# A gated MLP's width-3 convolution: its two neighbour terms moved from VectorE to GpSimd and one accumulating transfer, with one prefetch buffer given up

## The chip, the cores and the metric

The kernel runs on one NeuronCore of a Trainium2 chip. It is one launch, and the metric is the device time of that launch in microseconds (us). TensorE is PE in the profile (its weight loads are PEld), VectorE is DVE, ScalarE is ACT, GpSimd is POOL and SyncE is SP. A measurement of this kernel can tell about 0.2% (4.5 us) from no change.

## The reference

The model is two layers of a bidirectional encoder on 256 positions of width 2048, in float32. Each layer has a mixer (attention) and then a gated MLP, which is where the change lies:

```python
def conv_ffn(h, w_up, conv_w, conv_b, w_down):
    u = h @ w_up                                  # 256 x 2048 @ 2048 x 11264
    u = conv over positions, width 3, one 3-tap filter per channel, + conv_b
    gate, val = jnp.split(u, 2, axis=-1)          # 5632 channels each
    return (jax.nn.silu(gate) * val) @ w_down     # 5632 x 2048
```

So every channel's output at position t is `tap0*u[t-1] + tap1*u[t] + tap2*u[t+1] + bias`, with zeros outside. The change touches only how the terms of the two neighbours, t-1 and t+1, are formed and added.

## The kernel before

**Matmuls.** Every float32 operand is split in two parts of a shorter format, high and low, and each product is three matmuls (lines 135 to 137, or 189 to 191). The activations are the stationary side, and the weights stream as tiles of 128 x 512.

**The weight stream.** Weights come from HBM as tiles of 512 KB (`raw`, 128 x 1024 float32), issued on SP's queue. ScalarE rounds a tile to its high part (`wh`, line 147 or 182), VectorE subtracts to get the low part (`wl`, line 148 or 183). There are four `wh` and four `wl` buffers. One raw tile feeds twelve matmuls of `feed` (line 117): two row blocks of 128, two slices of the contraction, three products. `raw_tile` (line 104) hands out the raw buffers: four of the pool's own, and in some stages extra ones under a second tag. In the whole gated MLP, from the first pair of blocks on, `extra[0]` is `fp, ["raw2"]`, and every third tile comes from two `raw2` buffers. So six tiles can be held or in flight, and a load takes the buffer of the load six before it.

**Fast units.** Some slices of the contraction are done by `fast_unit` (line 167), a Strassen-like scheme with seven products in place of eight: it loads four raw tiles, adds and subtracts them on VectorE (line 181, four operations of 128 x 1024) and splits seven matrices (lines 182 and 183) for 42 matmuls. In the up-projection there is one such unit in the pairs 2, 4, 6 and 8 (`UP`). In the down-projection `pair` runs two units per pass, six in each layer, and there the sums are put in the `u` tiles. The first sum, `t1`, needs the unit's first and its fourth loaded tile.

**The MLP stage.** `ffn` (line 560) goes through eleven pairs of blocks in two halves (six and five pairs), each followed by a part of the down-projection. Of a pair, the gate block has 512 channels of the gate, the value block the 512 that it multiplies. A block's accumulators are scaled and copied out by ScalarE (`stg`, line 492), turned so that channels lie on partitions and positions on the free axis (`turned`, line 625: VectorE transposes 32 x 32 pieces into `quad`, then GpSimd copies eight pieces into `u` and ScalarE the other eight, line 632), and convolved by `conv` (line 609). There are three `u` tiles, one `cg` (gate result) and one `cv` (value result).

`conv` makes four ScalarE operations (line 612: `bias + tap1*u`, written to `c`) and then eight VectorE operations (line 620, 128 x 256 each: `c = tap*neighbour + c`, for two neighbours and four groups of channels). After both blocks are convolved, ScalarE takes the gate through SiLU (line 650) and VectorE multiplies gate and value (line 656). `act_split` (line 684) then splits the product for the down-projection.

**What sets the order.** The blocks' work is written as generators (`gate_gen`, line 642, and `value_gen`, line 658). `feed` advances one waiting generator by one `yield` after every few matmuls, so the work for one block is spread over the matmuls of the next. A scheduler then orders each engine's instructions by priority at build time, with the weight splits ahead (`high_priority`), and that order is fixed: an instruction that waits holds everything behind it on its engine.

The gate block of a pair is convolved in `value_gen` of that pair, the value block in `product`, from `gate_gen` of the next pair; the last pair of each half is convolved by `value_gen` and `flush`.

## Time and profile before

| | |
|---|---|
| timed runs | 2225.1 us median of 3 (2223.95 to 2225.7) |
| profiled execution, span from first to last instruction | 2220.5 us |
| PE matmul busy / PE weight loads busy | 2207.1 us (99%) / 1828.5 us (82%) |
| DVE busy | 1823.1 us (82%) |
| ACT busy | 1528.2 us (69%) |
| POOL busy | 546.1 us (25%) |
| HBM to SBUF and back, mean | 197 GB/s |

The page gives the profiled execution's span and no other time of it; the median of the timed runs lies 4.6 us above that span, which is what passes outside the first and last instruction. The stages of the MLP in the first layer are, by the starts of line 632: up-projection of the first half until about 535 us, its down-projection until about 650 us, the second half until about 875 us and its down-projection until about 960 us. In the second layer the MLP starts at about 1520 us and runs to the end.

How to read the views: a row of a timeline has the start, the length, the engine, the line, the operation, and in brackets how long the engine had been idle and what ended that. A row of the waits has who waited for whom, microseconds in total, how many times, and the longest. In a table by stretches each engine has its busy time and in brackets its number of instructions.

### The profile page before, as it was taken

The page shows a single profiled execution, that of the slowest core. Times are in us where ns is not written, and L with a number is a line of the kernel's source. Part 1 is how long each engine was busy: PE and PEld are TensorE (multiplying, and loading weights), DVE is VectorE, ACT ScalarE, POOL GpSimd, SP SyncE. Part 2 cuts the span into 40 slices and gives each one's busy share as a digit, 9 for nine tenths or more (in the row PEclk, how much of TensorE's full clock was granted, in tenths as well). Part 3 has the DMA queues.
Part 4 walks back from the last instruction along what each step waited for, and adds up shares of the span by engine and source line. Part 5 has one row for each costly group of instructions (what it writes and reads, how often), then busy time and mean ns, then how long its engine had stood idle before and what let it go on. Part 6 is the DMA issues. An engine that isn't in the chain of part 4 may idle for free.

```text
span 2220.5 us, 28992 instructions
## 1 busy us (share of the span) xinstructions
PE 2207.1 (99%) x9933; PEld 1828.5 (82%) x9933; DVE 1823.1 (82%) x2295; ACT 1528.2 (69%) x2328; POOL 546.1 (25%) x793
## 2 busy tenths in 40 slices
PE   9999999999999999999999999999999999999998
PEld 7888888888888888888888888888888888888887
DVE  6877669899897998868876878587798998879887
ACT  7666677787457787677756775567777855678764
POOL 3343222321003221042354216003222300212211
PEclk9999999999999999999999999999999999999999
DMA  8665665656656566665666555556555565656754
GB/s 305 192 220 184 216 188 190 201 189 196 203 181 222 186 205 200 204 202 195 183 199 199 174 180 189 190 184 214 181 202 194 192 209 190 217 162 218 224 193 143
DMA packets 126181, 439.60 MB, mean 198 GB/s; under 512 B 14408, under 2 KB 18248, under 8 KB 126032
## 3 DMA queue, kind: packets, MB, share of 16 engines
q1 hardware_dynamic: 123056, 429.05, 59.2%
q0 software_dynamic: 2688, 8.39, 1.5%
q8 instruction: 78, 1.28, 0.2%
q14 instruction: 71, 0.58, 0.1%
q10 hardware_dynamic: 288, 0.30, 0.0%
HBM read 432.34 MB, written 5.34 MB: 197 GB/s over the span
## 4 chain that ended last, share of the span: by engine, by line
PE 54%; POOL 1%; issue 1%; DMA 0%; ACT 0%; DVE 0%; POOLq 0%; DVEq 0%; ACTq 0%
PE acc L136 15%; PE acc L135 15%; PE acc L137 15%; PE ps L190 1%; PE ps L189 1%; PE ps L191 1%; PE acc L190 1%; PE acc L189 1%; PE acc L191 1%; DMA raw<-in_w_b_dram 0%; POOL wide L399 0%; PE ps L1422 0%; PE ps L342 0%; POOL wide L384 0%; ACT wh L147 0%
## 5 line engine op out<-in xcount | busy, mean ns | idle before, releaser
L148 DVE TENSOR_TENSOR wl<-raw,wh 128x1024 fp32r<-128x1024 f32 (+1 forms) x700 | 858.9, 1237 | 257.6 <-ACT wh L147 253.1
L147 ACT ACTIVATE wh<-raw 128x1024 fp32r<-128x1024 f32 (+1 forms) x700 | 726.8, 1046 | 342.5 <-PE acc L137 240.6
L136 PE MATMUL acc<-wl,xh 128*128 128x512 f32 x1984 | 773.8, 390 | 1.5 <-DVE wl L148 1.4
L135 PE MATMUL acc<-wh,xh 128*128 128x512 f32 x1984 | 773.7, 390 | 0.5 <-ACT wh L147 0.5
L137 PE MATMUL acc<-wh,xh 128*128 128x512 f32 x1984 | 772.1, 389 | 0.0
L136 PEld LDWEIGHTS acc<-wl,xh 128*128 128x128 f32 x1984 | 372.6, 188 | 81.5 <-DVE wl L148 5.7
L135 PEld LDWEIGHTS acc<-wh,xh 128*128 128x128 f32 x1984 | 372.5, 188 | 77.4 <-ACT wh L147 1.0
L137 PEld LDWEIGHTS acc<-wh,xh 128*128 128x128 f32 x1984 | 372.4, 188 | 76.9
L632 POOL COPY u<-quad 32x256 f32<-32x256 f32 x352 | 237.7, 675 | 702.5 <-DVE quad L380 684.4
L135 PE MATMUL acc<-wh,a 128*128 128x512 f32 x720 | 280.9, 390 | 0.0
L136 PE MATMUL acc<-wl,a 128*128 128x512 f32 x720 | 280.3, 389 | 0.0
L137 PE MATMUL acc<-wh,a 128*128 128x512 f32 x720 | 280.0, 389 | 0.0
L182 ACT ACTIVATE wh<-raw 128x1024 fp32r<-128x1024 f32 x140 | 148.5, 1061 | 122.4 <-PE acc L137 102.6
L183 DVE TENSOR_TENSOR wl<-raw,wh 128x1024 fp32r<-128x1024 f32 x140 | 166.9, 1218 | 6.3 <-ACT wh L182 5.8
L632 ACT ACTIVATE u<-quad 32x256 f32<-32x256 f32 x352 | 147.8, 420 | 23.2 <-DVE quad L380 18.7
L137 PEld LDWEIGHTS acc<-wh,a 128*128 128x128 f32 x720 | 135.1, 188 | 28.3 <-DVE a L331 0.2
L135 PEld LDWEIGHTS acc<-wh,a 128*128 128x128 f32 x720 | 135.2, 188 | 27.7
L136 PEld LDWEIGHTS acc<-wl,a 128*128 128x128 f32 x720 | 135.2, 188 | 27.6 <-DVE wl L148 0.3
L399 POOL COPY wide<-quad 32x256 f32<-32x256 f32 x88 | 54.8, 622 | 234.8 <-DVE quad L380 167.8
L492 ACT ACTIVATE stg<-acc,rstd 128x512 f32<-128x512 f32 x122 | 81.9, 685 | 32.9 <-PE acc L137 21.3
L384 POOL COPY wide<-quad 32x256 f32<-32x256 f32 x133 | 89.8, 675 | 41.4 <-DVE quad L380 32.0
L380 DVE STREAM_TRANSPOSE quad<-stg 128x512 f32<-128x512 f32 x112 | 75.7, 696 | 11.6 <-ACT stg L492 11.4
(318 smaller groups left out, 2444.5 us busy)
## 6 DMA issues: line engine op xcount, KB each, us to landing
raw<-in_w_up_dram SPq DMA_DIRECT2D x352, 512.0 KB, 4.6
raw<-in_w_down_dram SPq DMA_DIRECT2D x176, 512.0 KB, 4.6
raw<-in_w_b_dram SPq DMA_DIRECT2D x144, 512.0 KB, 4.6
raw<-in_w_bo_dram SPq DMA_DIRECT2D x48, 512.0 KB, 4.4
raw<-in_w_a_dram SPq DMA_DIRECT2D x40, 512.0 KB, 4.7
raw<-in_w_ao_dram SPq DMA_DIRECT2D x32, 512.0 KB, 4.5
raw<-in_w_a_dram SPq DMA_DIRECT2D x16, 256.0 KB, 5.8
there<-quad POOLq DMA_DIRECT2D x6, 512.0 KB, 3.7
```

What stands on the lines that cost most here:

```text
L135: nc.tensor.matmul(accs[m], xh, wh[:, j, :], start=st, stop=False)
L136: nc.tensor.matmul(accs[m], xh, wl[:, j, :], start=False, stop=False)
L137: nc.tensor.matmul(accs[m], xl, wh[:, j, :], start=False, stop=sp)
L147: nc.scalar.activation(wh[:, c], r[:, c], AF.Copy)
L148: newest[0] = nc.vector.tensor_tensor(wl[:, c], r[:, c], wh[:, c].bitcast(F32), ALU.subtract)
L182: nc.scalar.activation(wh, r, AF.Copy)
L183: newest[0] = nc.vector.tensor_tensor(wl, r, wh.bitcast(F32), ALU.subtract)
L380: nc.vector.transpose(quad[:, :, at, :], src.rearrange("p (x c t) -> p c x t", c=4, t=32))
L384: nc.gpsimd.tensor_copy(o[32 * c:32 * c + 32, :, 32 * q:32 * q + 32], quad[32 * q:32 * q + 32, c])
L399: nc.gpsimd.tensor_copy(dst, src)
L492: evac[0] = nc.scalar.activation(o[:, m, :], accs[m], AF.Copy, scale=rstd[:, m:m + 1])
L632: put(u[32 * c:32 * c + 32, :, :, 32 * q:32 * q + 32], quad[32 * q:32 * q + 32, c].rearrange("p (j m) t -> p j m t", m=2))
```

## The change

For 18 of the 22 blocks of each layer (all but the last pair of each half) the convolution is made in two parts.

- `conv_begun`, after the block has been turned (for a gate block after the product of the pair before, for a value block after the gate block's addition): the same four ScalarE operations; four GpSimd multiplications of 128 x 256 that write `tap0*u[t-1]` to a new tile `side` (one buffer, 512 KB over all partitions); one transfer issued on GpSimd's queue that adds `side` to `c` in SBUF; four GpSimd multiplications of 128 x 256, in place in `u`, by tap2.
- `conv_ended`, where the convolution used to be: one VectorE addition of 128 x 1024, `c + u[t+1]`.

The space for `side` comes from the weight stream: `raw2` has one buffer in place of two, and every fifth raw tile takes it in place of every third. So five tiles can be held or in flight in the MLP, and a load takes the buffer of the load five before it.

```diff
     def raw_tile():
         count[0] += 1
-        if extra[0] and count[0] % 3 == 0:
+        if extra[0] and count[0] % (3 if len(extra[0][1]) > 1 else 5) == 0:
             pool, tags = extra[0]
             tags.append(tags.pop(0))
-            return pool.tile([P, 2, 512], F32, tag=tags[0], name=nm("raw"), bufs=2 if len(tags) == 1 else 1)
+            return pool.tile([P, 2, 512], F32, tag=tags[0], name=nm("raw"))
         return spool.tile([P, 2, 512], F32, tag="raw", name=nm("raw"), bufs=NRAW)
...
+            def flat_of(u):
+                return u.rearrange("p j m t -> p j (m t)")
+
+            def conv_begun(blk):
+                n, u, c = blk
+                t = fp.tile([P, 4, NT], F32, tag="side", name=nm("side"))
+                flat = flat_of(u)
+                for j in range(4):
+                    tc.keep_in_program_order(nc.scalar.activation(
+                        halves(c[:, j]), u[:, j, :, :P], AF.Identity, bias=tap(n, j, 3), scale=tap(n, j, 1)))
+                    nc.gpsimd.tensor_scalar(halves(t[:, j]), halves(flat[:, j, :NT])[:, ::-1], tap(n, j, 0), None,
+                                            op0=ALU.mult)
+                    if j == 1:
+                        yield
+                nc.gpsimd.dma_start(c.rearrange("p j t -> p (j t)"), t.rearrange("p j t -> p (j t)"),
+                                    accum_op=ALU.add)
+                yield
+                for j in range(4):
+                    nc.gpsimd.tensor_scalar(flat[:, j, 1:NT + 1], flat[:, j, 1:NT + 1], tap(n, j, 2), None, op0=ALU.mult)
+
+            def conv_ended(blk):
+                n, u, c = blk
+                side = flat_of(u)[:, :, 1:NT + 1].rearrange("p j (m t) -> p j m t", m=2)[:, :, ::-1]
+                cv = c.rearrange("p j (m t) -> p j m t", m=2)
+                nc.vector.tensor_tensor(cv, cv, side, ALU.add)
+
...
                     with tc.issue_after(evac[0].ins):
                         nc.scalar.activation(value[3], value[3], AF.Silu)
-                    yield from product(value)
-
-            def product(value):
+                    yield from product(value, True)
+                if blk[0] + 1 not in (p for _, p in HALVES):
+                    yield from conv_begun(blk)
+
+            def product(value, begun=False):
                 n, u, cv, cg, _, _ = value
-                yield from conv((n, u, cv))
+                if begun:
+                    conv_ended((n, u, cv))
+                else:
+                    yield from conv((n, u, cv))
                 nc.vector.tensor_tensor(cv, cg, cv, ALU.mult)
 
             def value_gen(accs, blk, gate, last):
+                blk = blk[:3]
                 s = evac_scaled(fp, accs, rstd, 1)
...
-                yield from conv(gate)
+                conv_ended(gate)
+                yield from conv_begun(blk)
```

The order of the instructions on TensorE and on SP's queue stays as it was. On the other engines the pieces move; two places are shown, both around pair 4 of the first half in the first layer. In the names, `cg` and `cv` are the gate and value results, `u` the turned block, `quad` the transposed pieces, `wl` the low part of a weight tile, and `side` the first neighbour's product.

On VectorE, pair 4's gate and value convolutions, before:

```order
L148 TENSOR_TENSOR wl_4758<-raw_4753,wh_4757 128x1024
L620 SCALAR_TENSOR_TENSOR cg_4156<-u_2635,cw_555,cg_4156 128x256 x3
L148 TENSOR_TENSOR wl_4785<-raw_4755,wh_4784 128x1024
L620 SCALAR_TENSOR_TENSOR cg_4156<-u_2635,cw_555,cg_4156 128x256 x5
L148 TENSOR_TENSOR wl_4813<-raw_4808,wh_4812 128x1024
L380 STREAM_TRANSPOSE quad_4773<-stg_4748 128x16x32
L148 TENSOR_TENSOR wl_4832<-raw_4810,wh_4831 128x1024
L380 STREAM_TRANSPOSE quad_4773<-stg_4748 128x16x32
L620 SCALAR_TENSOR_TENSOR cv_4157<-u_2636,cw_555,cv_4157 128x256 x2
L148 TENSOR_TENSOR wl_4858<-raw_4853,wh_4857 128x1024
L148 TENSOR_TENSOR wl_4879<-raw_4855,wh_4878 128x1024
L620 SCALAR_TENSOR_TENSOR cv_4157<-u_2636,cw_555,cv_4157 128x256 x4
```

and with the change (L649 is the addition in `conv_ended`, L687 the product):

```order
L148 TENSOR_TENSOR wl_4799<-raw_4794,wh_4798 128x1024
L649 TENSOR_TENSOR cg_4188<-cg_4188,u_2635 128x1024
L148 TENSOR_TENSOR wl_4826<-raw_4796,wh_4825 128x1024
L148 TENSOR_TENSOR wl_4854<-raw_4849,wh_4853 128x1024
L649 TENSOR_TENSOR cv_4189<-cv_4189,u_2636 128x1024
L380 STREAM_TRANSPOSE quad_4814<-stg_4789 128x16x32 x2
L148 TENSOR_TENSOR wl_4873<-raw_4851,wh_4872 128x1024
L687 TENSOR_TENSOR cv_4189<-cg_4188,cv_4189 128x1024
```

The sixteen multiply-adds of the pair became two additions. The value block's addition now stands two weight splits behind the gate block's, and ahead of the transposes of the next block and of the fourth split; before, its first two multiply-adds stood behind that split and both transposes, and its last two three splits further on.

On GpSimd, the same stretch, before:

```order
L632 COPY u_2637<-quad_4182 32x8x32 x8
L632 COPY u_2635<-quad_4401 32x8x32 x8
L632 COPY u_2636<-quad_4578 32x8x32 x8
L632 COPY u_2637<-quad_4773 32x8x32 x8
L632 COPY u_2635<-quad_4957 32x8x32 x8
```

and with the change (L635 writes `side`, L639 is the accumulating transfer, L643 multiplies in place):

```order
L658 COPY u_2636<-quad_4617 32x8x32 x8
L643 TENSOR_SCALAR u_2635<-u_2635,cw_555 128x256 x3
L639 DMA cg_4188<-side_4572 128x1024
L643 TENSOR_SCALAR u_2635<-u_2635,cw_555 128x256
L635 TENSOR_SCALAR side_4723<-u_2636,cw_555 128x256 x4
L643 TENSOR_SCALAR u_2636<-u_2636,cw_555 128x256 x3
L639 DMA cv_4189<-side_4723 128x1024
L643 TENSOR_SCALAR u_2636<-u_2636,cw_555 128x256
L658 COPY u_2637<-quad_4814 32x8x32 x8
```

Between the copies of one block and the next now stand eight multiplications and a transfer's issue for each block; here the gate block's last part and all of the value block's follow the copies of the value block, and the value block's `side` takes the buffer that the gate block's transfer reads.

## The prediction

> **What bounds the kernel now.** I read the page's busy times first, then a table of stretches, then what the weight loads waited for.
>
> ```profile
> PE 2207.1 (99%) x9933; PEld 1828.5 (82%) x9933; DVE 1823.1 (82%) x2295; ACT 1528.2 (69%) x2328; POOL 546.1 (25%) x793
> 600.00:640.00 40.00, 40.00 (x178) 33.10 (x178) 35.77 (x33) 24.25 (x24) 0.32 (x3) 1.00 0.58 186
> 460.00:500.00 40.00, 39.94 (x176) 32.58 (x176) 40.00 (x61) 33.59 (x55) 13.98 (x16) 1.00 0.61 210
> 540.00:580.00 40.00, 39.74 (x175) 32.44 (x174) 36.09 (x35) 23.12 (x23) 0.00 (x0) 1.00 0.62 195
> PEld acc L136 <- DVE wl L148: 6.1, 14, 0.9
> PEld acc L136 <- DVE wl L148: 1.4, 2, 0.9
> PEld acc L136 <- DVE wl L148: 1.9, 5, 0.7
> ```
>
> The second row is a stretch of pure matmuls: 178 in 40 us, one each 0.225 us, at a granted clock of 1.00. Even where VectorE is busy all 40.00 us (third row) TensorE still gets 176. The last three rows are weight loads that waited for VectorE's splits: in the whole kernel 6.1 us, in the first layer's up-projection stretch (350 to 540 us) 1.4, and from 1515 to 2130 us, nearly all of the second layer's MLP, 1.9. So TensorE sets the time, VectorE is close behind, and what a relief of VectorE can give back in the convolution stages is about 1.4 + 1.9 us, less what of the 1.9 falls in the down-projection. I take 2 us. The question is what the change delays past the lead that the splits have over the matmuls.
>
> **What is removed and added on the engines.**
>
> ```profile
> L620 DVE SCALAR_TENSOR_TENSOR cg<-u,cw,cg 128x256 f32<-128x256 f32 x176 | 79.3, 501 | 0.1
> L620 DVE SCALAR_TENSOR_TENSOR cv<-u,cw,cv 128x256 f32<-128x256 f32 x176 | 77.0, 486 | 1.8 <-ACT cv L612 1.4
> L656 DVE TENSOR_TENSOR cv<-cg,cv 128x1024 f32<-128x1024 f32 x22 | 27.2, 1237 | 0.5
> L632 POOL COPY u<-quad 32x256 f32<-32x256 f32 x352 | 237.7, 675 | 702.5 <-DVE quad L380 684.4
> L632 POOL COPY u<-quad x352: 392/473/2408, 296.5 to 2112.9; 32x256 f32<-32x256 f32 x176
> L1067 POOL TENSOR_TENSOR t<-stg,st_q 128x256 f32<-128x256 f32 x16 | 18.0, 1148 | 16.7 <-ACT stg L492 16.7
> 377.65 7.40 POOL L632 COPY u<-quad 32x256 f32<-32x256 f32 x8 [26.75 <-DVE quad L380]
> 383.37 1.41 DVE L148 TENSOR_TENSOR wl<-raw,wh 128x1024 fp32r<-128x1024 f32 x1
> 386.89 1.21 DVE L148 TENSOR_TENSOR wl<-raw,wh 128x1024 fp32r<-128x1024 f32 x1
> there<-quad POOLq DMA_DIRECT2D x6, 512.0 KB, 3.7
> oc<-in_onehot_dram POOLq DMA_DIRECT2D x1, 512.0 KB, 5.0
> L1171 POOL DMA_DIRECT2D there<-quad x6 | 3.6, 607 | 6.7 <-DVE quad L380 5.6 <-DVE mx L1121 1.0
> ```
>
> 36 blocks change. VectorE loses 36 x 8 multiply-adds of 0.494 us, 142 us, and gains 36 additions priced like the product, 1.24 us, 45 us. GpSimd gains 288 multiplications of 128 x 256. No such operation is in the trace. From below bounds it the copy of as many elements, 0.39 us at its shortest; from above the two-input operation, 1.15 us; the copy's mean of 0.675 lies between. I take **0.5 us**, since for most of the time that counts below VectorE is itself waiting. GpSimd and VectorE hinder each other: while copies run (377.65 to 385.05) a split takes 1.41 us, and 1.21 just after. At 0.2 us each, 288 multiplications cost VectorE 58 us at most, so it still comes out 39 us lighter.
>
> The Trainium skill's page "SBUF — State Buffer", section "SBUF: two separate sides", goes further: GpSimd and a VectorE operation with two SBUF inputs hold the shared port pair exclusively, and the loser fully blocks. [...]
>
> The transfer moves 512 KB from SBUF to SBUF and also reads its target; no row has an accumulation. Nearest are two 512 KB transfers on GpSimd's queue, 3.7 and 5.0 us to landing. I take **5.0**, the one that writes SBUF; it may as well be 3.7, or 8 if reading the target costs as much again. Its issue holds GpSimd 0.6 us. ScalarE's work stays the same.
>
> **Term one: the additions stand too early.** In the old form the multiply-adds needed only `u` and ScalarE's four operations. Now VectorE's addition waits for four multiplications, three more that stand ahead of the transfer, its issue and its landing. Every weight split behind it waits too. The first place is pair 4's value block:
>
> ```profile
> 482.99 7.39 POOL L632 COPY u<-quad 32x256 f32<-32x256 f32 x8 [12.72 <-DVE quad L380]
> 498.16 1.22 DVE L148 TENSOR_TENSOR wl<-raw,wh 128x1024 fp32r<-128x1024 f32 x1
> 499.30 0.70 DVE L380 STREAM_TRANSPOSE quad<-stg 128x512 f32<-128x512 f32 x1
> 499.93 1.18 DVE L148 TENSOR_TENSOR wl<-raw,wh 128x1024 fp32r<-128x1024 f32 x1
> 503.99 0.39 PE L136 MATMUL acc<-wl,xh 128*128 128x512 f32 x1
> ```
>
> `u` is whole at 490.4, or at 489.5 with the lighter VectorE. Then GpSimd does 3 multiplications (gate), issue, landing (`side` has one buffer), 4 and 3 multiplications (value), issue, landing: 10 x 0.5 + 2 x 0.6 + 2 x 5.0 = 16.2, so 505.7. The addition (1.24), two transposes (1.40) and the split (1.18, with gaps 1.9) follow: 510.2. The matmul that needs this split ran at 503.99. TensorE waits **6.2 us**; with 0.4 and 3.7 it waits about 1.5, with 0.675 and 8 about 14. Twice in the kernel, once a layer: 12.4.
>
> The second place is the first gate block of a second half:
>
> ```profile
> 676.54 7.36 POOL L632 COPY u<-quad 32x256 f32<-32x256 f32 x8 [40.87 <-DVE quad L380]
> 686.57 1.23 DVE L148 TENSOR_TENSOR wl<-raw,wh 128x1024 fp32r<-128x1024 f32 x1 [0.24 <-ACT wh L147]
> 693.66 0.39 PE L136 MATMUL acc<-wl,xh 128*128 128x512 f32 x1
> ```
>
> The copies end at 683.9; 7 x 0.5 + 0.6 + 5.0 gives 693.0, addition and split 695.5, against 693.66: **1.8 us** late, zero at the quick values, 6 at the slow ones; twice, 3.6. The other 32 blocks are mostly like the gate block of pair 3:
>
> ```profile
> 413.82 5.31 POOL L632 COPY u<-quad 32x256 f32<-32x256 f32 x8 [9.34 <-DVE quad L380]
> 428.14 2.36 DVE L148 TENSOR_TENSOR wl<-raw,wh 128x1024 fp32r<-128x1024 f32 x2
> 431.49 0.39 PE L136 MATMUL acc<-wl,xh 128*128 128x512 f32 x1
> ```
>
> Its addition stands ahead of the split of 428.14. Copies end at 419.1, plus 9.1 is 428.2, the addition and the split end at 430.7, and the matmul came at 431.49: just hidden, and 2.2 us late with 8 us to landing. For all 32 together I put 3 us, up to 20 at the slow values (eight or nine at such a price). Sum **19 us**, bounds 3 to 60.
>
> **Term two: one raw buffer less.** The fast units of the down-projection need their fourth load at once:
>
> ```profile
> DVE u L181 <- DMA raw<-in_w_down_dram: 20.9, 9, 3.5
> 551.38 5.22 DVE L148 TENSOR_TENSOR wl<-raw,wh 128x1024 fp32r<-128x1024 f32 x4
> 553.91 0.85 SPq L170 DMA_DIRECT2D raw<-in_w_down_dram  x1
> 560.11 1.22 DVE L181 TENSOR_TENSOR u<-raw,raw 128x1024 f32<-128x1024 f32 x1 [3.51 <-DMA raw<-in_w_down_dram]
> 567.05 1.22 DVE L183 TENSOR_TENSOR wl<-raw,wh 128x1024 fp32r<-128x1024 f32 x1
> 568.33 0.50 PE L190 MATMUL acc<-wl,s 128*128 128x512 f32 x1 [0.26 <-DVE wl L183]
> ```
>
> Four splits run back to back, 1.3 us apart; the second ends at 553.9 and frees the buffer six loads back, and SP issues the unit's fourth load at 553.91. VectorE's first sum waits for it 3.51 us, until 560.11, and the unit never recovers: its third split ends at 568.27 and the matmul behind it starts at 568.33. With the buffer five loads back, the load is issued behind the third split, 1.3 us later, and TensorE waits 1.3 us more. In nine of the twelve units the first sum already waits for this load (first row). The shift is 1.3 us where splits run back to back and 12 x 0.225 = 2.7 where the matmuls pace them, about 2 on average; the smallest lead in the units, read like the last two rows, is 0.05 to 1.8 us, about 0.8 on average. So 12 x 1.2 = 14 us; a load issued later has fewer beside it (this one took 6.2 us to use, the median for this tensor is 4.6 to landing), so I take **12 us**, bounds 0 and 23 (12 x (2.7 - 0.8)). In the up-projection's units the loads behind the unit come later too, but had several us to spare; nothing there.
>
> **Sum.** 19 + 12 - 2 = 29 us on this execution's span of 2220.5, so a span of about 2249; with the 4.6 us outside it **2254 us**, 1.3% slower.
>
> By the Trainium skill's "DMA: Bandwidth & Descriptors", section "Anatomy of one DMA — SWDGE (gpsimd) path", such a transfer takes about 2.0 us plus bytes over 436 GB/s, 3.2 us here (an estimate); the first place would then be 2.6 us late, the second not at all, and the sum 2240.
>
> **Rivals.**
> - *Only the buffer counts.* Multiplications take 0.4 us and the transfer 3.7: term one is 2 x 1.5 + 1 = 4, the sum +14, 2239 us. For it: VectorE is lighter, and the copies' minimum is 0.39. Against: the accumulation has more to do than the row with 3.7.
> - *The transfer is slow*, 8 us: term one is 2 x 14 + 2 x 6 + 20 = 60, the sum +70, 2295 us. For it: it reads two tiles and shares the engines with weights (DMA share 0.6 in the stretches). Against: both rows are below 5.1.
> - *Nothing is lost.* The place is the first one: from 489.5 to 499.5 there are 10 us for two landings and ten multiplications, so it decides at about 3.1 us to landing with 0.25 us each; and the later loads land as early as before, since fewer share the engines. Then only the 2 us are left: 2223 us, same or barely faster. For it: the load at 553.91 took 6.2 us with two more behind it. Against: no row has a multiplication or landing that short.
> - *Faster beyond measurement* would need more than 4.5 us, and the waits above do not hold that much, unless matmuls themselves came closer than 0.225 us, which no row suggests.
>
> **How the numbers follow.** Forecast 0.48, only the buffer 0.25, slow transfer 0.13, nothing lost 0.11, faster 0.03. The likeliest case's own range is 2240 to 2268. The range for 8 in 10 reaches through the second case down and part of the third up: 2228 to 2285. A measurement tells about 0.2%, 4.5 us, from no change; the first three cases are slower by more, less a little for a milder second case: slower 0.84, same 0.12, faster 0.04.
>
> **What would show it.** In the changed profile: VectorE's busy time near 1780 us and GpSimd's up by 140 us or more; the weight loads' waits for splits grow from 6 to some 30 us; VectorE's additions wait several us for the transfer or for GpSimd, longest at pair 4's value block; the first sums of the down-projection's units wait for loads in all twelve units and longer in total than 20.9. If the transfer lands in under 4 us and VectorE never waits for it, term one is wrong; if the sums' waits stay near 21 us, term two is. A loss in stages without a convolution or a fast unit would be a mechanism that I have not seen.

## The result, and the profile after

The changed kernel takes 2436.6 us (median of 3 runs, 2435.7 to 2442.8) against 2225.1: the ratio is 1.0958, with a 95% interval of 1.0938 to 1.0978. It is slower, as forecast, but by 212 us and not by 29.

The page of the changed kernel, the line of busy times:

```profile
PE 2281.0 (94%) x9933; PEld 1867.4 (77%) x9933; DVE 1751.5 (72%) x2043; ACT 1528.1 (63%) x2328; POOL 961.0 (39%) x1117
```

And the view of its cores, the span and the mean granted clock:

```profile
core 0: 2434.9 us, clock 0.969
```

Before, the span was 2220.5 with TensorE busy for 2207.1 of it. The span has grown by 214.4 us: 73.9 of it as busy time of TensorE (the same 9933 matmuls take longer) and 140.5 as its idle time. The mean granted clock, 0.969 over 2434.9 us against 0.999 over 2220.5 before, accounts for about 73 us by itself, so the growth of the busy time is the lower clock. VectorE is 72 us lighter, where 39 were forecast, and nothing came of it. GpSimd is 415 us heavier, where 140 were forecast.

Who waits for what (engine, what it waited for: us in total, times, longest):

```profile
DVE cg L649 <- DMA cg<-side: 124.9, 18, 8.9
DVE cv L649 <- DMA cv<-side: 113.0, 17, 9.9
PEld acc L136 <- DVE wl L148: 155.4, 56, 7.8
PE acc L136 <- DVE wl L148: 133.7, 42, 7.3
DVE u L181 <- DMA raw<-in_w_down_dram: 23.7, 11, 3.7
```

The groups of GpSimd's multiplications (busy us, mean ns of one, then the idle time before them):

```profile
L635 POOL TENSOR_SCALAR side<-u,cw 128x256 f32<-128x256 f32 x144 | 219.8, 1542 | 28.6 <-DMA cg<-side 14.3 <-DMA cv<-side 9.1 <-issue 1.9
L643 POOL TENSOR_SCALAR u<-u,cw 128x256 f32<-128x256 f32 x144 | 185.4, 1298 | 33.2 <-ACT cv L633 25.5 <-DVE acc L551 7.1
```

And the view of the tile that the transfer reads (shortest, median and longest of the first neighbour's multiplications in ns, and of the transfer's time from issue to landing in us):

```profile
L635 POOL TENSOR_SCALAR side<-u,cw x144: 916/1439/3009, 303.7 to 2288.5; 128x256 f32<-128x256 f32 x144
DMA to landing us min/median/max: 4.4/5.9/9.1
```

VectorE's wide additions wait for the transfer in 35 of 36 blocks, 238 us in all, and the weight loads that waited 6.1 us for VectorE's splits before now wait 155 (a weight load and its matmul wait for the same split, so the two rows are not added). One multiplication takes 1.5 and 1.3 us on average, never under 0.916.

The place that the prediction counted as just hidden is pair 3's gate block. Its rows on GpSimd, VectorE and TensorE in the changed kernel (start, length, what it waited for):

```profile
447.43 5.26 POOL L658 COPY u<-quad 32x256 f32<-32x256 f32 x8 [9.01 <-DVE quad L380]
452.78 5.74 POOL L635 TENSOR_SCALAR side<-u,cw 128x256 f32<-128x256 f32 x4
458.50 3.76 POOL L643 TENSOR_SCALAR u<-u,cw 128x256 f32<-128x256 f32 x3
462.21 0.88 POOL L639 DMA_DIRECT2D cg<-side  x1
467.15 1.23 DVE L649 TENSOR_TENSOR cg<-cg,u 128x1024 f32<-128x1024 f32 x1 [7.48 <-DMA cg<-side]
468.29 3.49 DVE L148 TENSOR_TENSOR wl<-raw,wh 128x1024 fp32r<-128x1024 f32 x3
469.56 0.80 PE L136 MATMUL acc<-wl,xh 128*128 128x512 f32 x1 [3.97 <-DVE wl L148]
470.58 0.63 PE L135 MATMUL acc<-wh,xh 128*128 128x512 f32 x1
```

Seven multiplications stand between the copies' end (452.69) and the transfer's issue: 9.5 us where 3.5 were forecast. VectorE has nothing else that may go first; it stands for 7.48 us, with three splits behind it, and TensorE waits 4 us. A matmul behind that wait (last row) is listed with 0.63 us instead of 0.39.

The stretches around this place and one of the down-projection (us; busy time and count of TensorE, its weight loads, VectorE, ScalarE, GpSimd; granted clock, DMA share, GB/s):

```profile
448.00:452.00 4.00, 4.00 (x11) 3.05 (x10) 1.79 (x2) 3.87 (x9) 3.75 (x7) 0.50 0.65 205
452.00:465.00 13.00, 13.00 (x59) 10.78 (x58) 4.89 (x4) 9.28 (x12) 11.94 (x11) 0.99 0.60 188
470.00:473.00 3.00, 3.00 (x9) 2.31 (x9) 3.00 (x4) 0.00 (x0) 0.00 (x0) 0.56 0.62 193
2000.00:2040.00 40.00, 40.00 (x178) 33.11 (x178) 34.27 (x39) 19.20 (x19) 0.00 (x0) 1.00 0.62 205
```

For some 3 to 6 us after a wait the granted clock is 0.50 to 0.56 and matmuls stand 0.427 us apart. The down-projection (last row) is as before. Matmul by matmul against the trace of before, 206 of the 214 us arise in the up-projections. So nearly the whole loss lies in the convolution's stages, and it has two parts: TensorE waits for splits behind late additions, and each longer wait is followed by slowed matmuls.

### The profile page after: what moved, and what is told of

Read it like the earlier page. It is cut to its first block, busy times and chain, and to the rows that moved or that the text cites. A ratio compares the mean times of both kernels' runs of the same rounds, so it can differ in the third digit from the quotient of the medians.

```text
span 2434.9 us, 29284 instructions
## 1 busy us (share of the span) xinstructions
PE 2281.0 (94%) x9933; PEld 1867.4 (77%) x9933; DVE 1751.5 (72%) x2043; ACT 1528.1 (63%) x2328; POOL 961.0 (39%) x1117
## 5 line engine op out<-in xcount | busy, mean ns | idle before, releaser
L136 PE MATMUL acc<-wl,xh 128*128 128x512 f32 x1984 | 803.8, 405 | 133.7 <-DVE wl L148 133.7
L135 PE MATMUL acc<-wh,xh 128*128 128x512 f32 x1984 | 794.6, 401 | 3.0 <-ACT wh L147 2.9
L137 PE MATMUL acc<-wh,xh 128*128 128x512 f32 x1984 | 794.5, 400 | 0.0
L136 PEld LDWEIGHTS acc<-wl,xh 128*128 128x128 f32 x1984 | 386.7, 195 | 233.6 <-DVE wl L148 154.4
L135 PEld LDWEIGHTS acc<-wh,xh 128*128 128x128 f32 x1984 | 386.1, 195 | 87.5 <-ACT wh L147 4.9
L137 PEld LDWEIGHTS acc<-wh,xh 128*128 128x128 f32 x1984 | 387.2, 195 | 80.6
L658 POOL COPY u<-quad 32x256 f32<-32x256 f32 x352 | 231.7, 658 | 430.5 <-DVE quad L380 417.6
L635 POOL TENSOR_SCALAR side<-u,cw 128x256 f32<-128x256 f32 x144 | 219.8, 1542 | 28.6 <-DMA cg<-side 14.3
L643 POOL TENSOR_SCALAR u<-u,cw 128x256 f32<-128x256 f32 x144 | 185.4, 1298 | 33.2 <-ACT cv L633 25.5
L399 POOL COPY wide<-quad 32x256 f32<-32x256 f32 x88 | 52.3, 594 | 238.3 <-DVE quad L380 171.3
L649 DVE TENSOR_TENSOR cg<-cg,u 128x1024 f32<-128x1024 f32 x18 | 22.1, 1225 | 124.9 <-DMA cg<-side 124.9
```

The costliest lines, as they stand in the source:

```text
L135: nc.tensor.matmul(accs[m], xh, wh[:, j, :], start=st, stop=False)
L136: nc.tensor.matmul(accs[m], xh, wl[:, j, :], start=False, stop=False)
L137: nc.tensor.matmul(accs[m], xl, wh[:, j, :], start=False, stop=sp)
L399: nc.gpsimd.tensor_copy(dst, src)
L635: nc.gpsimd.tensor_scalar(halves(t[:, j]), halves(flat[:, j, :NT])[:, ::-1], tap(n, j, 0), None, op0=ALU.mult)
L643: nc.gpsimd.tensor_scalar(flat[:, j, 1:NT + 1], flat[:, j, 1:NT + 1], tap(n, j, 2), None, op0=ALU.mult)
```

## Experiments

The table gives the time, the ratio to the kernel before with its interval, what TensorE's busy and idle time grew by against the profile of before (2207.1 and 13.4 us), and the idle time of VectorE ahead of the wide additions.

| kernel | us | ratio, 95% interval | busy + | idle + | additions' waits |
|---|---|---|---|---|---|
| the change | 2436.6 | 1.0958 (1.0938 to 1.0978) | 73.9 | 140.5 | 237.9 |
| raw ring alone | 2235.5 | 1.0047 (1.0034 to 1.0059) | 6.0 | 7.4 | none there |
| only the wide addition | 2231.2 | 1.0044 (1.0029 to 1.0059) | 3.6 | 6.1 | 22.7 |
| multiplications nobody reads | 2261.4 | 1.0165 (1.0149 to 1.0181) | 16.7 | 22.6 | none there |
| no multiplications | 2344.9 | 1.0532 (1.0515 to 1.0549) | 39.9 | 74.2 | 142.7 |
| no transfer | 2346.2 | 1.0545 (1.0530 to 1.0559) | 46.4 | 77.1 | 129.2 |
| no accumulation | 2296.0 | 1.0343 (1.0324 to 1.0361) | 25.2 | 48.5 | 98.5 |
| transfer issued first | 2377.4 | 1.0702 (1.0686 to 1.0718) | 51.0 | 107.4 | 186.4 |
| multiplications on ScalarE | 2357.7 | 1.0612 (1.0594 to 1.0629) | 49.8 | 89.9 | 112.0 |
| one wide multiplication | 2377.5 | 1.0697 (1.0681 to 1.0712) | 58.2 | 99.5 | 87.9 |
| additions held, gate's later | 2349.6 | 1.0570 (1.0554 to 1.0586) | 46.8 | 79.3 | 128.8 |
| the same, issued first | 2319.0 | 1.0424 (1.0407 to 1.0441) | 36.1 | 63.9 | 100.6 |
| the same, value's two parts later | 2276.5 | 1.0243 (1.0226 to 1.0260) | 17.8 | 36.3 | 63.6 |
| the same, value's three parts later | 2271.7 | 1.0218 (1.0203 to 1.0233) | 19.2 | 30.6 | 38.9 |

Four of these kernels leave out a part of the result: the ones with only the wide addition, without multiplications, without accumulation, and with three parts. The last three columns are of the profiled execution, which for the kernel without multiplications took 2336.4 us. In the smaller rows `busy +` is not slowed matmuls alone: with the multiplications that nobody reads it is 16.7 us, at a mean granted clock of 0.998. The stalls, at the end of this section, are a measurement by themselves.

**The ring alone**: does one raw buffer less cost 12 us?

```diff
-        if extra[0] and count[0] % 3 == 0:
+        if extra[0] and count[0] % (3 if len(extra[0][1]) > 1 else 5) == 0:
...
-            return pool.tile([P, 2, 512], F32, tag=tags[0], name=nm("raw"), bufs=2 if len(tags) == 1 else 1)
+            return pool.tile([P, 2, 512], F32, tag=tags[0], name=nm("raw"))
```

> The kernel before with one part of the change alone: one buffer less in the ring of raw weight tiles; convolution as before. Theory of the prediction (term two): the fast units' fourth load is issued 1.3 to 2.7 us later and TensorE waits for it, +12 us, 2237 us, and VectorE's first sums wait longer for their loads than the 20.9 us of before, in all twelve units. Rival, from the profile of the changed kernel (these waits are 23.7 us there, and the down-projection's stretches have 177 to 178 matmuls in 40 us as before): the load behind has enough to spare, 2223 to 2228 us.

It costs 10.5 us (7.6 to 13.1, from the interval). But not where it was put. The fast units' sums wait no longer than before, 20.8 us in 11 places. The weight loads' wait in the first layer's up-projection (330 to 540 us), where before had 1.4 us, is this:

```profile
PEld acc L136 <- DVE wl L148: 4.6, 6, 1.4
```

In the waits of the whole kernel, ScalarE's wait for the up-projection's loads was 21.7 us before:

```profile
ACT wh L147 <- DMA raw<-in_w_up_dram: 25.7, 18, 4.0
DVE u L181 <- DMA raw<-in_w_down_dram: 20.8, 11, 2.4
```

**Neither multiplications nor transfer, only the wide addition**: is one addition for a whole block late by itself?

```diff
-                t = fp.tile([P, 4, NT], F32, tag="side", name=nm("side"))
...
-                    nc.gpsimd.tensor_scalar(halves(t[:, j]), halves(flat[:, j, :NT])[:, ::-1], tap(n, j, 0), None,
-                                            op0=ALU.mult)
...
-                nc.gpsimd.dma_start(c.rearrange("p j t -> p (j t)"), t.rearrange("p j t -> p (j t)"),
-                                    accum_op=ALU.add)
...
-                for j in range(4):
-                    nc.gpsimd.tensor_scalar(flat[:, j, 1:NT + 1], flat[:, j, 1:NT + 1], tap(n, j, 2), None, op0=ALU.mult)
```

> The changed kernel with neither multiplications nor transfer: ScalarE's four operations and one wide VectorE addition of the unscaled second neighbour; the first neighbour's term and the second's scaling are not computed. Theory: the wide addition and its place cost nothing by themselves, since ScalarE's four operations end some 3 us after they begin and VectorE arrives at the addition 5 us after that beginning in the profiles so far; what is left is the raw buffer: 2228 to 2245 us. Rival: one addition for the whole block in place of eight short operations that alternate with the weight splits is itself late or too long in one piece, 2260 us or more.

2231.2 us, the ratio of the ring alone. The wide addition is free, VectorE's 77 us of relief (1746.4 us busy) buys nothing, and the whole rest of the loss, some 200 us, hangs on the multiplications and the transfer.

**Multiplications that nobody reads**: what do they cost beside others, if no one waits for them?

```diff
+                t = fp.tile([P, 4, NT], F32, tag="side", name=nm("side"))
+                flat = u.rearrange("p j m t -> p j (m t)")
+                for i in (0, 2):
+                    for j in range(4):
+                        nc.gpsimd.tensor_scalar(halves(t[:, j]), halves(flat[:, j, i // 2:i // 2 + NT])[:, ::-1],
+                                                tap(n, j, i), None, op0=ALU.mult)
```

> The kernel before with one raw buffer less, as in the change, and with the eight multiplications of every convolution done on GpSimd as well, into a tile that nobody reads (in 44 blocks, 352 of them); the convolution itself stays on VectorE as before. Theory A (they cost because VectorE's addition waits for them): 2225 to 2250 us. Theory C (they cost by sharing SBUF with VectorE, which here is even busier than in the change): 2350 us or more. Each of them should be about 0.92 us where VectorE is idle and longer beside it; how much longer VectorE's multiply-adds (0.49 us before) and splits (1.22) become is the price of the sharing.

2261.4 us: 26 us beyond the ring, for 352 of them. The old multiply-adds beside them take 0.589 us instead of 0.486:

```profile
L626 DVE SCALAR_TENSOR_TENSOR cv<-u,cw,cv 128x256 f32<-128x256 f32 x176 | 95.7, 589 | 0.4
```

That is a price, above theory A's 2250 and far below theory C's 2350. Work on GpSimd that nobody waits for explains little of the 212 us.

**No multiplications, and no transfer**, each alone. In the first the tile of zeros is filled once a layer, and both neighbours' multiplications are taken out as in the diff above:

```diff
-                t = fp.tile([P, 4, NT], F32, tag="side", name=nm("side"))
+                t = zero_side()
```

> The changed kernel without its GpSimd multiplications; the transfer adds a tile of zeros instead, and the wide addition adds the unscaled neighbour, so the two neighbours' terms are not computed. Theory A, the multiplications' length is what was mis-sized (some 1.4 us where 0.5 was taken): copies to addition is then about four operations of ScalarE (2.4 us), issue 0.9 and landing 5.7, 9 us, which the prediction found just hidden, so nearly all is back: 2225 to 2245 us. Theory B, the transfer is what costs (it has to read its target, and VectorE stands behind it): most stays, 2330 us or more. Theory C, GpSimd's multiplications slow VectorE's and others' work by sharing SBUF, whoever waits for them: 2225 to 2245 us as well; told apart from A by the kernel in which nobody reads the multiplications.

```diff
-                nc.gpsimd.dma_start(c.rearrange("p j t -> p (j t)"), t.rearrange("p j t -> p (j t)"),
-                                    accum_op=ALU.add)
+                sides.append(t)
...
+                nc.vector.tensor_tensor(c, c, sides.pop(0), ALU.add)
                 nc.vector.tensor_tensor(cv, cv, side, ALU.add)
```

> The changed kernel with the transfer replaced by a second wide VectorE addition; all multiplications stay on GpSimd. Theory A (multiplications' length): copies to addition is then 8 x 1.4 = 11.2 us in place of 16.4, and VectorE has 1.2 us more, so of the 7.3 us by which a block is late some 3 stay: about 2310 to 2350 us. Theory B (the transfer's landing): nearly all is back, 2225 to 2250 us. Theory C (multiplications hinder VectorE): as the changed kernel or slower, 2420 to 2470 us.

2344.9 and 2346.2 us. The first lies in the range of the theory that the transfer is the cause, the second in that of the theory that the multiplications are: either run alone would have named a cause. Taking either away wins back about 91 us, not nearly all and not nothing; both theories, that one of them is the cause, fall. The chain of waits had to be read again. Pair 3's gate block in the kernel without multiplications:

```profile
428.91 5.29 POOL L662 COPY u<-quad 32x256 f32<-32x256 f32 x8 [11.25 <-DVE quad L380]
437.72 1.08 ACT L641 ACTIVATE cg<-u,cw 128x256 f32<-128x256 f32 x2
439.10 0.86 POOL L645 DMA_DIRECT2D cg<-side  x1 [4.90 <-ACT cg L641]
447.52 1.23 DVE L653 TENSOR_TENSOR cg<-cg,u 128x1024 f32<-128x1024 f32 x1 [6.52 <-DMA cg<-side]
449.94 0.68 PE L136 MATMUL acc<-wl,xh 128*128 128x512 f32 x1 [3.17 <-DVE wl L148]
```

The transfer is issued 4.9 us after the copies' end (434.20), where the change has 9.5, and yet the addition comes 13.3 us after it, where the change has 14.5. What was won ahead of the issue, the landing gave back: 8.4 us from issue to addition against 4.9. The views of the transfers show the landing. First the stretch of the change (455 to 470 us), then that of the kernel without multiplications (436 to 448): the hardware queue's packets (the weight loads: count, MB, share of the engines), and the transfer's landing.

```profile
q1 hardware_dynamic: 443, 1.61, 31.5%
cg<-side POOLq DMA_DIRECT2D x1, 512.0 KB, 4.8
```

```profile
q1 hardware_dynamic: 446, 1.61, 44.3%
cg<-side POOLq DMA_DIRECT2D x1, 512.0 KB, 8.3
```

Over all 36 transfers of this kernel (the view of the tile again):

```profile
DMA to landing us min/median/max: 4.5/8.2/9.7
```

An earlier transfer runs among the weight loads, and its median landing is 8.2 us against 5.9 in the change. The two stretches hold the same 1.61 MB of loads and differ in length, so their shares prove little by themselves. Counted for each of the change's 36 transfers while it is under way, the loads' share of the engines is at most 0.21 for the fifteen that land within 5.1 us and 0.63 to 0.73 for the four that take over 8 us. In the change VectorE mostly stands still while the transfer is under way, so no split frees a raw buffer and fewer loads are in flight beside it. That a busy VectorE itself holds the transfer up is not borne out: in the kernel without multiplications five land in 4.5 to 4.9 us with VectorE busy for 63 to 94% of that time.

**No accumulation**: the same kernel with a plain copy.

```diff
-                nc.gpsimd.dma_start(c.rearrange("p j t -> p (j t)"), t.rearrange("p j t -> p (j t)"),
-                                    accum_op=ALU.add)
+                nc.gpsimd.dma_start(c.rearrange("p j t -> p (j t)"), t.rearrange("p j t -> p (j t)"))
```

> The kernel without multiplications (2345 us) with a plain copying transfer of the zeros in place of the accumulating one, so the block's own terms are overwritten as well. There the additions waited 8.4 us from the transfer's issue, against 5.0 us in the changed kernel. Theory A, it is the accumulation, which also reads its target: about 4 us to landing as in the two 512 KB rows of before, the waits of 143 us fall to about a third, 2265 to 2300 us. Theory B, it is the weight loads in flight, with which an earlier transfer shares the engines (in the changed kernel they had run dry while VectorE waited): landing as long as with accumulation, 2325 to 2350 us.

2296.0 us: theory A's range. The median landing is 6.1 us against 8.2, so accumulating costs some 2 us a transfer here. Theory A's 4 us to landing is not reached; the loads in flight are the likely other part.

**The transfer issued first**, ahead of the second neighbour's multiplications (`put` is the transfer):

```diff
-                for j in range(4):
-                    nc.gpsimd.tensor_scalar(flat[:, j, 1:NT + 1], flat[:, j, 1:NT + 1], tap(n, j, 2), None, op0=ALU.mult)
+                with tc.issue_after(put.ins):
+                    for j in range(4):
+                        nc.gpsimd.tensor_scalar(flat[:, j, 1:NT + 1], flat[:, j, 1:NT + 1], tap(n, j, 2), None, op0=ALU.mult)
```

> The changed kernel with the transfer issued ahead of the four multiplications of the second neighbour; in the changed kernel three of them stand ahead of it on GpSimd. Theory A (landing is as slow as in the kernel without multiplications when it is issued earlier, 8.4 us from issue): the addition comes 4.1 + 8.4 = 12.5 us after ScalarE's first operation in place of 12.8, so nearly all of the loss stays, 2410 to 2440 us. Theory B (landing stays at 5 us): the addition then waits for the second four multiplications, 4.1 + 0.9 + 4 x 1.4 = 10.6 us, 2.2 us sooner in 36 blocks, about 80 us and some of the slowed matmuls behind the waits: 2330 to 2365 us.

2377.4 us, between the two: 59 us better than the change. The median landing went from 5.9 to 7.2 us and so ate a part of what the earlier issue gave.

**Another engine and another shape for the multiplications.** The diffs show the first neighbour; the second is changed likewise.

```diff
-                    nc.gpsimd.tensor_scalar(halves(t[:, j]), halves(flat[:, j, :NT])[:, ::-1], tap(n, j, 0), None,
-                                            op0=ALU.mult)
+                    nc.scalar.activation(halves(t[:, j]), halves(flat[:, j, :NT])[:, ::-1], AF.Copy, scale=tap(n, j, 0))
```

> The changed kernel with the eight multiplications of each block on ScalarE instead of GpSimd, 0.59 us each as its conv operations are in the profile, so 288 of them put 170 us on ScalarE. Theory A (GpSimd's multiplications were mis-sized, and the landing is the rest): a block's four plus four operations end 5.5 to 6 us after the first, then issue and landing of 5 to 8.4 us give 11 to 14 us against 12.8: 2340 to 2420 us. Rival (GpSimd's sharing of SBUF with VectorE is most of the price): no GpSimd multiplication is left, 2340 us or less. Second rival (ScalarE's weight roundings behind the multiplications become late): above 2440 us.

```diff
-                    nc.gpsimd.tensor_scalar(halves(t[:, j]), halves(flat[:, j, :NT])[:, ::-1], tap(n, j, 0), None,
-                                            op0=ALU.mult)
...
+                taps = cw[:, 16 * n:16 * n + 4].unsqueeze(2).to_broadcast([P, 4, NT]).rearrange("p j (m t) -> p j m t", m=2)
+                src = flat[:, :, :NT].rearrange("p j (m t) -> p j m t", m=2)[:, :, ::-1]
+                nc.gpsimd.tensor_tensor(t.rearrange("p j (m t) -> p j m t", m=2), src, taps, ALU.mult)
```

> The changed kernel with each neighbour's four GpSimd multiplications as one two-input multiplication of 128 x 1024 (the four taps broadcast along the row); the transfer's issue then stands behind the first of them alone. Such an operation is not in the traces; a two-input one of 128 x 256 took 1.15 us there, so the estimate is 4 x 1.15 = 4.6 us or less, against 4 x 1.4 = 5.6 for the four. Theory (only lengths and order count): like the kernel with the transfer issued first or somewhat better, 2330 to 2385 us. Rival (a two-input operation on GpSimd stops VectorE for its whole length): 2400 us or more, with splits beside it much longer than 1.4 us.

On ScalarE they take 0.496 us each, and the time is 2357.7 us: theory A's range. With no GpSimd multiplication left, more than half of the loss stays (the first rival said 2340 or less), and the additions still wait 112.0 us for the transfer. One wide multiplication takes 1.9 us at its shortest, about half of what four take, and the additions wait only 87.9 us; but the time is 2377.5, in the theory's range and no better than with the four multiplications and the transfer issued first. The split's row of this kernel and of the kernel without multiplications:

```profile
L148 DVE TENSOR_TENSOR wl<-raw,wh 128x1024 fp32r<-128x1024 f32 (+1 forms) x700 | 930.7, 1343 | 278.1 <-ACT wh L147 274.1
```

```profile
L148 DVE TENSOR_TENSOR wl<-raw,wh 128x1024 fp32r<-128x1024 f32 (+1 forms) x700 | 857.7, 1238 | 278.4 <-ACT wh L147 274.2
```

VectorE's busy time is 1847.4 us against 1744.8 in the kernel without multiplications: 103 us for 72 operations, 1.4 us apiece. Of the 700 splits 42 take over 1.6 us, in the median 3.3; without multiplications five do, and none over 1.8. That is the sign that the rival named, and the likely reason why the shorter waits bring no gain; no run separates it. The change's 288 operations with one input cost VectorE 7 us in all (1751.5 against 1744.8), and it is they that stretch, from 0.92 to 1.4 us.

**Later additions**: is VectorE simply brought to the addition too early? Here multiplications and transfer are as in the change. Each addition is tied behind a weight split (`newest` is the split written last), and the gate block's is written behind the value block's first part.

```diff
-                nc.vector.tensor_tensor(cv, cv, side, ALU.add)
+                with tc.issue_after(newest[0].ins):
+                    nc.vector.tensor_tensor(cv, cv, side, ALU.add)
...
+                yield from conv_begun(blk)
                 conv_ended(gate)
-                yield from conv_begun(blk)
```

> The changed kernel with its additions later in VectorE's order: each is tied behind the newest weight split, and the gate block's addition is written behind the value block's first part; multiplications and transfer are as in the change. In VectorE's order two splits and more stand between the old and the new place of most of them (110 to 114, 121 to 135, 155 to 176 splits ahead of the addition; a few, 138 and 149, move by one or two). Theory, that VectorE is held by an addition that comes up too early: of 238 us of waits less than 80 are left, and the time is below 2310 us. Rival, that the additions are late for the Silu, the product and the next pair's block as well, or that multiplications and transfers cost by what they take from other engines: the loss moves, 2380 us or more.

> The same, and the transfer issued ahead of the second neighbour's four multiplications. Theory: the chain is 2 to 4 us shorter and the addition later, so waits of a few us in all, and what is left is the raw buffer (10 us) and GpSimd's sharing with VectorE (26 us for 352 multiplications in the kernel in which nobody reads them, 21 for 288): 2245 to 2275 us. Rival as for the run before: 2340 us or more.

```profile
DVE cv L650 <- DMA cv<-side: 109.6, 14, 9.8
DVE cg L650 <- DMA cg<-side: 19.1, 4, 8.5
```

The first of the two takes 2349.6 us, between theory and rival. Its rows show why: the gate blocks' waits went from 124.9 to 19.1 us, the value blocks' stayed at 109.6 (113.0), because the value additions moved by two splits at most, where 16 of the 18 gate additions moved by two to 21; the time fell by 87 us. Issued first as well it is 2319.0, above that theory's 2275: value blocks again, 86.6 us. Two more kernels move these alone, by two parts as here and by three:

```diff
-                    for _ in range(1 if blk[0] not in UP else 4 if value[5] // 4 - 1 in fast else 3):
+                    for _ in range(2 + (1 if blk[0] not in UP else 4 if value[5] // 4 - 1 in fast else 3)):
```

> The kernel with held additions and the transfer issued first (2319 us), and the product of the value block, with its addition, two parts of the program later; two splits more, 2.7 us each, then stand ahead of most value additions (116 to 119, 140 to 140, 150 to 152, 177 to 178, 185 to 187). There 84.5 us of 98.5 us of waits are left at value additions, in 14 places. Theory (VectorE is held by additions that come up before their transfer): these waits halve, and the time goes to 2265 to 2295 us. Rival (moving the value addition delays the product, the next gate block and its chain as much): 2305 us or more.

> The same with three parts; most value additions have three to four splits more ahead of them (119, 141, 153, 179, 188), 8 to 11 us. Theory: hardly any wait for a transfer is left; what stays is the raw buffer (10 us) and GpSimd's sharing with VectorE (up to 21 us): 2245 to 2275 us. Rival as in the run before: 2305 us or more.

2276.5 and 2271.7 us: both in the theory's range. But with three parts some of the values are handed on to the down-projection before their product is formed, so that kernel computes something else, and only the one with two parts counts for what follows. The waits, of the run with two parts:

```profile
DVE cv L651 <- DMA cv<-side: 43.1, 10, 8.5
DVE cg L651 <- DMA cg<-side: 14.6, 2, 7.5
```

So 160 of the 212 us come back with all 288 multiplications and all 36 accumulating transfers in place, by moving nothing but when they are issued and when VectorE asks for their sum (the value block's product moves with it). Of the 54 us that remain, the ring has 10; the rest goes with the 64 us of waits that are left and with the sharing, and was not taken further apart.

**Stalls**: do slowed matmuls come with a wait wherever it is?

```diff
+STALL = {60: 6, 68: 7, 76: 8, 84: 9, 92: 10, 100: 11, 560: 6, 568: 7, 576: 8, 584: 9, 592: 10, 600: 11}
...
-                    newest[0] = nc.vector.tensor_tensor(wl[:, c], r[:, c], wh[:, c].bitcast(F32), ALU.subtract)
+                    for _ in range(STALL.get(nsplit[0], 1)):
+                        newest[0] = nc.vector.tensor_tensor(wl[:, c], r[:, c], wh[:, c].bitcast(F32), ALU.subtract)
```

> The kernel before, with twelve weight splits in the mixers' stages, far from any convolution, done 6 to 11 times over (same result), so that TensorE waits there between about 1 and 8 us. In the changed kernel, waits up to 2.2 us are followed by at most a few matmuls at twice the spacing, and most waits over 2.3 us by 6 to 13 of them, 1.2 to 2.6 us more. Theory, that the wait itself brings the lower clock: the same here, with a granted clock of 1.00 in stretches whose waits are short and lower ones where they are long. Rival, that it comes from the convolution's traffic: no slowed matmuls here whatever the wait.

The first six splits fell in the mixer, ahead of the first convolution (its first copy starts at 350 us); the other six fell in the second layer's MLP and are not used here. The matmul after one of the waits:

```profile
238.08 0.79 PE L137 MATMUL acc<-wl,a 128*128 128x512 f32 x1 [7.00 <-DVE wl L151]
```

Stretches behind this wait, further on, and behind one of 11.9 us (granted clock third from the right):

```profile
238.00:244.00 6.00, 5.92 (x18) 4.72 (x19) 2.17 (x4) 3.64 (x8) 3.15 (x8) 0.69 0.50 175
244.00:256.00 12.00, 12.00 (x54) 9.95 (x53) 9.61 (x13) 7.92 (x15) 0.00 (x0) 1.00 0.52 169
274.00:280.00 6.00, 6.00 (x16) 4.70 (x17) 0.46 (x1) 1.06 (x1) 0.00 (x0) 0.56 0.23 87
```

Behind waits of 7.0 and 11.9 us the clock is 0.69 and 0.56 over 6 us, and 1.00 in between: the wait brings the lower clock, not the convolution. Behind a shorter one, 1.54 us at 171.8, the matmuls keep their usual spacing. By the starts of its matmuls, 12 are slowed behind the wait of 11.9 us, and 6 to 13 behind the change's waits of 4 to 5 us: the extra price does not grow with the wait.

## Why the prediction was wrong, step by step

- **What bounds the kernel: held.** TensorE sets the time. VectorE's busy time came to 1751.5 us (forecast 1780), and the kernel with only the wide addition shows that this is worth nothing.
- **The multiplication, 0.5 us: this step failed.** It lies above the bound I had set (1.15 us, a two-input operation): 0.916 us at its shortest, 1.44 and 1.20 us in the median of the two lines. Bounds from a copy and from a two-input operation did not enclose an operation with one input and a tap per partition. With seven ahead of an issue the mistake counts seven times: 9.5 us for 3.5 at pair 3's gate block.
- **What they take from VectorE, at most 58 us: held as a bound.** It was 7 us in the change, 20 in the kernel with two parts (1764.5 us busy against 1744.8 without multiplications), and 45 for 352 of them beside the old multiply-adds (1867.2 against 1821.7 with the ring alone). The rule of the Trainium skill that the prediction names ("SBUF — State Buffer", section "SBUF: two separate sides"), that the loser fully blocks, would make it 144 us at 0.5 us a multiplication (an estimate); for these operations no run shows that. For two-input ones it comes close: 1.4 us lost on VectorE for an operation of 1.9 to 2.2.
- **The transfer, 5.0 us: near as an average and wrong as a constant.** Counted from the start of its issue it landed after 4.4 to 9.1 us, median 5.9, where 0.6 + 5.0 were forecast. At pair 3's gate block the sum of term one, done again with the measured lengths, gives 9.5 + 0.9 + 4.1 = 14.5 us from the copies' end to the addition, against 9.1; with the 0.8 us to spare it makes TensorE 4.6 us late, and it waited 4.0. So the way of reckoning was right, its first size wrong.
- **Term one, 19 us: mis-sized, and this decided the forecast.** It came to 133 us of idle time (140.5 less the ring's 7.4), seven times as much. The four places that I had priced one by one, pair 4's value block and the first gate block of the second half in each layer, in TensorE's timeline of the change:

```profile
563.68 0.80 PE L136 MATMUL acc<-wl,xh 128*128 128x512 f32 x1 [6.37 <-DVE wl L148]
...
763.13 0.79 PE L136 MATMUL acc<-wl,xh 128*128 128x512 f32 x1 [5.03 <-DVE wl L148]
...
1920.27 0.79 PE L136 MATMUL acc<-wl,xh 128*128 128x512 f32 x1 [7.33 <-DVE wl L148]
...
2119.20 0.80 PE L136 MATMUL acc<-wl,xh 128*128 128x512 f32 x1 [5.27 <-DVE wl L148]
```

  Pair 4's value block, 6.2 us forecast, cost 6.37 and 7.33, but by accident: its chain took 24.7 us (copies' end 535.4, addition 560.1), not 16.2, and TensorE had already paid 4.2 of it at the gate block before. The first gate block of the second half, 1.8 forecast, cost 5.03 and 5.27. "The other 32 blocks ... 3 us" is where the loss is: idle time grew by 140.5 us; less these four places (24.0) and the ring's 7.4, some 109 us are theirs. I had found one of them just hidden and let it stand for all, and a longer chain then cost in nearly every block. The length of the multiplications is not the whole of it: without any of them 120 us of the loss stay. One sum was wrong too: with 0.4 and 3.7 us the first place comes out 2.6 us late (4 + 1.2 + 7.4 = 12.6 against 16.2), not 1.5, and the rival "only the buffer counts" near 2241 us, not 2239; no conclusion hangs on that.
- **A term was missing.** 73.9 us of the loss are matmuls slowed by the lower clock behind the waits, and the sum had none, though it forecast waits of 6 us. The rule stands in the Trainium skill: "TensorE: Matmul & The Clock Gate", section "Part 1: The HAM clock gate (the "warmup" mystery)", says that the clock is halved after an idle window of about 3.4 us and released after as long a busy one. The traces agree with the half rate (0.427 us between starts) and with the length (the low stretches last 3.41 us or twice that behind the change's waits), but not with the idle window, as the last section shows; I had not weighed it.
- **Term two, 12 us: right in size, 10.5, and wrong in place.** The extra waits are mostly in the up-projection, which I had given "nothing there". The sign I had named, longer waits of the down-projection's sums in all twelve units, did not come (20.8 us in 11 places, and 23.7 in 11 in the change, against 20.9 in 9), and read by itself would have called the term wrong.
- **The rivals.** "Only the buffer counts" and "nothing is lost" are excluded. "The transfer is slow" had a true part, a landing of 8 us among weight loads; but in the change itself only 4 of 36 took over 8 us, and its 2295 was still 140 us too low.

## What to carry to other kernels

The relief of an engine that was not the bound bought nothing here, and a chain put in its place (multiply, issue, land, add) cost its length wherever an in-order engine reached its end early: look for where the consumer stands in its order, and move it down there before anything is made faster. Where one block is "just hidden", price the other thirty at the upper bound of the step that repeats, since an error there is multiplied by its count. And a wait of TensorE over some 2 us is to be priced with the slowed matmuls behind it, about 1.7 us for each step of 3.41 us at half clock.

## What the runs showed of the hardware

- **Slowed matmuls after a wait.** In the traces of the change and of all fourteen experiments, leaving out waits that begin within 6 us behind another, TensorE's waits between matmuls (the idle time in brackets) were followed by four or more matmuls 0.42 us or more apart in none of 87 waits of 0.8 to 1.5 us, 15 of 53 of 1.5 to 2.0, 45 of 63 of 2.0 to 3.0, 23 of 27 of 3.0 to 3.5 and 79 of 81 longer ones, with some 9 such matmuls on average. A good part of the clock drops came after waits shorter than the 3.4 us of the passage named above.
- **Why waits of equal length differ.** In every trace with more than one of them, the low stretches of the granted clock start on a grid of 3.41 us, and in the change those behind a wait last one step or two. Three steps around the addition of pair 3's gate block (TensorE's busy time stands behind the comma; granted clock third from the right):

```profile
465.91:469.32 3.41, 0.00 (x0) 0.00 (x0) 2.17 (x2) 1.13 (x2) 0.00 (x0) 0.99 0.12 22
469.32:472.73 3.41, 3.17 (x8) 2.52 (x9) 3.41 (x5) 0.00 (x0) 0.00 (x0) 0.51 0.50 154
472.73:476.15 3.42, 3.42 (x17) 2.81 (x16) 2.62 (x3) 2.28 (x4) 1.88 (x3) 1.00 0.73 252
```

  After a step at full clock with less than 1.6 us of idle TensorE the next was never lowered (10297 steps of all 16 traces, the kernel before included), after one with 2.1 us or more always (136), in between in 40 of 78. So it counts how much of a wait falls within one step: the same wait in the mixer, at 143 us, is 1.97 us long in the kernel before, and no matmul is slowed; it is 1.98 in the change, and seven are.
- **GpSimd beside VectorE.** A multiplication by a scalar per partition (128 x 256, one input) takes 0.92 us at its shortest and mostly gives way: 1.2 to 1.4 us in the median, up to 3.0, with 7 us lost on VectorE for 288 of them in the change. Beside VectorE's multiply-adds of 128 x 256 they cost it 45 us for 352. A two-input one (128 x 1024) takes 1.9 us at its shortest and 2.2 on average, and VectorE loses 1.4 us to each.
- **A 512 KB transfer from SBUF to SBUF on GpSimd's queue** lands after 4.4 to 9.1 us in the change, and it goes with what else is in flight: within 5.1 us where weight loads took at most 0.21 of the engines' time, over 8 where they took 0.63 to 0.73. Accumulating adds about 2 us to the median (8.2 against 6.1).
